# Ten input products of the mixing stage take raw weights and the normalised residual, in whole F32

## The chip, the cores and the metric

The kernel runs on one core of one Trainium2 chip, as one program. The metric is the device time of one execution in microseconds (us), and of several executions the median. The engines are named as the profile names them: PE multiplies matrices, PEld is PE's loading of the stationary operand, DVE, ACT and POOL work element by element, SP issues most of the DMA transfers.

## The reference, cut to what matters

One inference step of a decoder trunk with two layers, on 256 prompt tokens and 8 x 4 sample tokens; the kernel treats these 288 tokens as one set (NT = 288). A layer is

```python
x  = LN(alpha*x + 0.5*SwiGLU_1(x))            # ffn1, width 2816
z  = x @ W_in                                 # 1024 x 3584, the mixing stage's input product
z_rw, z_hg, z_cm = split(z, [1024, 1024 + 2048])
o  = concat[rwkv7(z_rw), hgrn2(z_hg), chunk_gmlp(z_cm)] @ W_out
x  = LN(alpha*x + o)
x  = LN(alpha*x + 0.5*SwiGLU_2(x))            # ffn2
...
q, fz, i, og = split(z_hg, 4)                 # HGRN2: 4 heads of 128 features
f = lb + (1 - lb)*sigmoid(fz);  log_f = log(max(f, 1e-30));  k = 1 - f
o = linear recurrence of silu(q), k, i, log_f;  o = rms(o)*norm_g*silu(og)
u, v = split(z_cm, 2)                         # gMLP: gelu(u), layer norm of gelu(v), causal mix
```

All of it is in float32. HGRN2's recurrence decays by products of f over tokens, so its inputs are wanted precisely.

## The kernel before

Activations lie feature-major: eight chunks of 128 features, each [128, 288]. A dense product yields 256 output features at a time, two PSUM accumulators `d` of [128, 288] (or 290 columns). Its weights come in blocks of 512 x 256 (`raw`, 512 KB, one DMA by SP at L347). W_in is fourteen such products of two blocks in each layer: four for RWKV (`rw_z`, called z here), and ten "background products" for HGRN2 and the gMLP: f, q, v, o with two each and cu, cv.

**Split products.** PE multiplies in F32R, a reduced form of float32. To keep precision, `prep` (L338) splits each block: ACT copies `raw` to `wh` in F32R, and DVE (for some blocks POOL) subtracts to get the low part `wl`. The moving side is split likewise into x-high and x-low (`newx`). `block` (L374) then issues three matmuls for each 128 x 128 piece (chunk k, column half c): wl by x-high, wh by x-high, wh by x-low. One product of 256 columns has 16 pieces, so 48 matmuls. `weights` keeps two blocks prepared ahead.

**The norm is applied after the product.** The product's operand x is (u - m) g, not yet divided by the deviation. `zfix` (L449) applies the norm to each result: it copies two extra columns (`cc<-d`), multiplies by the tokens' 1/deviation (`y<-d,rho`), and adds the shift (`y<-nu,cc,y`), all on DVE; sigmoid, gelu or copy on ACT and the gate on DVE follow, with cc as bias. The norm's output itself (`ax`, times ALPHA, for the residual sum after mixing) is made by `residual_g` (L696): per chunk `ax<-ax,rho` and `ax<-ax,nu` on DVE and `ax<-ax,ga` on ACT.

**Order.** The tile framework places each engine's instructions in one in-order stream by priority: trace order less the credit that `prio` gives (`PR`, L1782). In `mix` (L1689) the four z products come first. Then `go` runs the chains of `CHAINS` (L1778) in rounds: `pre` and `prompt` (RWKV for the prompt: decay, keys, a blocked inverse with doubling sizes), `sample`, `scan` (HGRN2's decay products with the matrices hA), `hmix`, `hsam`, `cm`, and others. After each step of a chain, `fill` takes a step (two pieces) of the background products, in the order `ORDER = ('f1', 'q0', 'f0', 'q1', 'cu', 'v1', 'cv', 'v0', 'o1', 'o0')`. `residual_g` is a chain of its own, `res`, last in the rounds. After the chains comes the output product (`mix_w_out`), split as the others, whose operand chunks 2 to 5 need HGRN2's results `hgO`.

**Who splits.** `PLO = {'z': (), 'f': (0,), 'q': (0,), 'v': (1,), 'c': (0,), 'o': (0,)}` names the blocks whose low part POOL makes: one of the two blocks of every background product, so ten a layer. Buffers: three each of `raw`, `wh`, `wl`, four PSUM banks `d`.

Names met below: `shp` transposes the token shift of RWKV, `pb` sums the squares of keys (from `rn`), `pD`, `pE`, `pR` belong to the prompt's inverse, `pns`, `poS` to the samples, `hot` turns HGRN2's outputs to feature-major, `cO` is the gMLP's mix (from `cM`), `hs` loads HGRN2's carried sample states (SP, L1523), `plg` is a small plain F32 product of the gate's lora.

Of the kernel before, what the change touches and what calls it, by code (L numbers as in the profile page):

```python
# [38 lines left out]
class Trunk:  # L39
# [80 lines left out]
    def consts(self):  # L120
# [34 lines left out]
        # causal masks over [s, t]: t > s and t >= s  # L155
# [5 lines left out]
        # block-merge masks: ml[b][t, s] and mt[b][s, t]  # L161
# [13 lines left out]
        # the same for blocks of 64 tokens, in rows of (block parity, token)  # L175
# [19 lines left out]
        # sample block masks over [(h,s), (h,t)], blocks of four tokens  # L195
# [9 lines left out]
        # the same with the rows of head h at the place of head (h + 2) % 4  # L205
# [3 lines left out]
        # row -> batch within a 32-token group, and row -> parity of its head  # L209
# [10 lines left out]
        # sums over a head's 64 rows into 32 equal rows, and their spreading back  # L220
# [11 lines left out]
        # a token's row in each group of 32; minus one at odd rows  # L232
# [3 lines left out]
        # two heads' inclusive sample blocks in either half of the rows  # L236
# [17 lines left out]
        # a token's row in each group of 32, for either pair of heads  # L254
# [3 lines left out]
        # the first four rows repeated for each batch  # L258
# [3 lines left out]
        # token -> batch, and a token's row in each group of 32  # L262
# [4 lines left out]
        # reset points of the running sums: token 0 of each chunk  # L267
# [70 lines left out]
    def prep(self, spec):  # L338
        """A block of weights, loaded and split into high and low parts."""
# [15 lines left out]
    @staticmethod  # L355
    def blocks(w, n0, nk, pool=()):
        return [(*w, tuple(range(k, min(k + 4, nk))), n0, i in pool) for i, k in enumerate(range(0, nk, 4))]
# [16 lines left out]
    def block(self, spec, x, res, first, last):  # L374
        """A block's share of a product."""
# [13 lines left out]

    def dense_g(self, w, n0, x, nk, pool, res):  # L390
# [11 lines left out]
    def dense_by(self, w, n0s, x, groups):  # L402
        """Several products, each group of chunks through all of them before the next."""
# [7 lines left out]
    def fill(self, n=1):  # L411
        """Goes on with the products in the background by n steps."""
# [18 lines left out]
    def hilo(self, r, name, n=NT):  # L431
        """Rows of high and low parts in turn, of equal rows."""
# [5 lines left out]
    def newx(self, nt):  # L438
        """Operand tiles of a product's moving side: eight 128-row chunks, high and low parts."""
# [9 lines left out]
    def zfix(self, ps, st, nm):  # L449
        """A product's two column blocks, and their biases, with the norm's scale (and shift) applied."""  # L450
# [148 lines left out]
    def final(self, po, m6, coef, g, square, i):  # L599
        """The last norm, in rows of tokens, and the outputs; the last rows are the prompt's end and the samples."""  # L600
# [6 lines left out]
        def rows(j, c):  # L607
            """A chunk, times the norm's gain, in rows of tokens."""
# [40 lines left out]
        # the mean's rest as rows of high, low and high parts  # L649
# [34 lines left out]
    def final_load(self, l):  # L684
        """The last norm's shift in each row, and its gain in (negated) rows of high, high and low parts."""
# [10 lines left out]
    def residual_g(self, pend):  # L696
        """The norm's output itself, times ALPHA for the next residual sum."""
# [9 lines left out]
    def residual_x(self):  # L707
        """The same, and operand tiles of it."""
        x = self.newx(NT)
        for c, _ in enumerate(self.residual_g(self.ln_pend)):  # L710
            self.act(x[0][c], self.ax[:, c])
            self.sub(x[1][c], self.ax[:, c], x[0][c].bitcast(F32), self.eng("xl"))
        return x

# [5 lines left out]
    def load_x(self, specs):  # L720
        """The operand tiles of the inputs; both loads in halves of the features, and the first weights between."""
# [24 lines left out]
    def rw_z(self, l, q, x, st):  # L746
# [41 lines left out]
    def rw_pre(self, l, q, zs):  # L788
# [3 lines left out]
        # lora products  # L792
# [3 lines left out]
        else:  # L796
            # tanh(x) = 2 sigmoid(2 x) - 1
# [19 lines left out]
        # running sums of the log decay (in units of -exp(-0.5)), centred in each chunk  # L817
# [17 lines left out]
        # keys  # L835
# [459 lines left out]
    def unit(self, l, n0, x, st, nm, fin):  # L1295
# [4 lines left out]
        for c in range(2):  # L1300
            fin(c, y[c], cb[c])
# [531 lines left out]
```

## Time and profile before

| what | value |
|---|---|
| median of 3 runs (lowest, highest) | 1374.07 us (1373.8, 1381.42) |
| span of the profiled execution | 1379.8 us |
| mean granted clock of PE | 0.969 |
| busy: PE, PEld, DVE, ACT, POOL | 1308.3, 1255.1, 1009.8, 663.8, 274.1 us |
| mixing stage of layer 0, from the first z product to the output product's end | 234 to 486 us |
| the same of layer 1 | 911 to 1155 us |

The span runs from the first to the last instruction of the profiled execution; the page gives no further time of its own for it, and it lies between the lowest and the highest of the three runs. An engine is busy while one of its arithmetic instructions runs. The granted clock is the share of PE's full clock that the throttle let it have (1.00 is 2.4 GHz, 0.50 is 1.2 GHz).

### The profile page before, as it was taken

What the parts mean: (1) busy time and instruction counts of PE and PEld (TensorE: products, weight loads), DVE (VectorE), ACT (ScalarE), POOL (GpSimd) and SP (SyncE); (2) the same over time, 40 slices, a digit from 0 to 9 for tenths busy, and PEclk for the clock granted to TensorE, in tenths of its full rate; (3) what the DMA queues carried; (4) which work ended last, traced back from release to release, by engine and by line L of the source; (5) the groups of instructions that cost most, each with busy time, mean ns of one, the idle gap of its engine ahead of it and who ended that gap; (6) DMA issues with size and microseconds to landing.
All of it is one profiled execution on the core that took longest, in us unless ns stands there. A gap on an engine that the chain in (4) does not pass through costs nothing.

```text
span 1379.8 us, 27635 instructions
## 1 busy us (share of the span) xinstructions
PE 1308.3 (95%) x11161; PEld 1255.1 (91%) x11162; DVE 1009.8 (73%) x1844; ACT 663.8 (48%) x1052; POOL 274.1 (20%) x381
## 2 busy tenths in 40 slices
PE   7999999898987999999999999998889889999998
PEld 6999999877876999999999999997778789999997
DVE  3555448977877998774698775599986889977643
ACT  4454435762345554443465443368333645544433
POOL 9200001435554100000100000033464421000002
PEclk9999999987997999999999999999999889999999
DMA  5655554531123655554455555554212544555551
GB/s 175 187 168 168 162 165 150 154 106 34 48 86 113 187 156 158 165 168 153 155 168 167 167 156 161 167 160 131 78 31 71 149 124 145 168 161 161 175 168 58
DMA packets 208158, 194.12 MB, mean 141 GB/s; under 512 B 15911, under 2 KB 206363, under 8 KB 208030
## 3 DMA queue, kind: packets, MB, share of 16 engines
q1 hardware_dynamic: 207326, 190.91, 44.9%
q0 software_dynamic: 608, 1.31, 0.4%
q8 instruction: 88, 1.44, 0.4%
q14 instruction: 40, 0.33, 0.1%
q10 hardware_dynamic: 96, 0.13, 0.1%
HBM read 185.10 MB, written 7.22 MB: 139 GB/s over the span
## 4 chain that ended last, share of the span: by engine, by line
PE 79%; DVE 14%; issue 3%; ACT 2%; POOL 1%; DMA 0%; POOLq 0%; SPq 0%; DVEq 0%; ACTq 0%
PE d L97 71%; DVE wl L65 2%; DVE hgO L77 1%; ACT wh L62 1%; DVE yrw L77 1%; DVE hgQ L77 1%; PE pA L97 1%; DVE hR L65 1%; DVE hAT L94 1%; PE hO L97 0%; PE hA L97 0%; DVE ax L65 0%; PE pD L97 0%; POOL hgP L65 0%; DVE hL L65 0%
## 5 line engine op out<-in xcount | busy, mean ns | idle before, releaser
L97 PE MATMUL d<-x,wh 128*128 128x290 f32 (+1 forms) x3968 | 824.0, 301 | 2.5 <-DVE x L77 2.5
L97 PEld LDWEIGHTS d<-x,wh 128*128 128x128 f32 x3968 | 653.3, 192 | 9.8 <-DVE x L77 4.3
L97 PE MATMUL d<-x,wl 128*128 128x290 f32 (+1 forms) x1984 | 602.5, 304 | 16.2 <-ACT x L62 12.4
L62 ACT ACTIVATE wh<-raw 128x1024 fp32r<-128x1024 f32 x344 | 357.2, 1039 | 456.1 <-PE d L97 312.1
L65 DVE TENSOR_TENSOR wl<-raw,wh 128x1024 fp32r<-128x1024 f32 x324 | 395.1, 1220 | 239.4 <-ACT wh L62 238.1
L97 PEld LDWEIGHTS d<-x,wl 128*128 128x128 f32 x1984 | 380.5, 192 | 21.5 <-ACT x L62 15.5
L97 PE MATMUL d<-h,wh 128*128 128x288 f32 x1408 | 282.0, 296 | 0.0
L97 PEld LDWEIGHTS d<-h,wh 128*128 128x128 f32 x1408 | 226.2, 188 | 0.2
L97 PE MATMUL d<-h,wl 128*128 128x288 f32 x704 | 207.8, 295 | 0.0
L65 POOL TENSOR_TENSOR lnv<-lnq,lnq 128x288 f32<-128x288 f32 x6 | 8.2, 1375 | 848.7 <-ACT lnq L62 848.7
L97 PEld LDWEIGHTS d<-h,wl 128*128 128x128 f32 x704 | 132.5, 188 | 0.2
L65 POOL TENSOR_TENSOR wl<-raw,wh 128x1024 fp32r<-128x1024 f32 x20 | 50.0, 2502 | 66.3 <-ACT wh L62 66.3
L62 ACT ACTIVATE h<-sg 128x288 fp32r<-128x288 f32 x88 | 38.1, 435 | 24.5 <-DVE sg L65 20.9
L62 ACT ACTIVATE sg<-yg,ccg 128x288 f32<-128x288 f32 x66 | 34.3, 528 | 29.9 <-DVE yg L77 29.9
L62 ACT ACT_TABLE_LOAD x37 | 47.5, 1283 | 1.4 <-PEq L1821 0.8
L65 DVE TENSOR_TENSOR h<-sg,h 128x288 fp32r<-128x288 f32 x88 | 39.6, 452 | 5.6 <-ACT h L62 5.6
L77 DVE SCALAR_TENSOR_TENSOR ax<-d,ax 128x288 f32<-128x288 f32 x48 | 21.4, 452 | 29.4 <-PE d L97 29.4
L77 DVE SCALAR_TENSOR_TENSOR yu<-nu,ccu,yu 128x288 f32<-128x288 f32 x66 | 33.9, 514 | 0.8
L77 DVE SCALAR_TENSOR_TENSOR yg<-nu,ccg,yg 128x288 f32<-128x288 f32 x66 | 33.8, 515 | 0.8
L62 ACT ACTIVATE lnq<-ax 128x288 f32<-128x288 f32 x48 | 20.9, 435 | 26.2 <-DVE ax L77 26.0
L77 DVE SCALAR_TENSOR_TENSOR sg<-yu,ccu,sg 128x288 f32<-128x288 f32 x66 | 33.3, 509 | 0.0
L65 DVE TENSOR_TENSOR yu<-d,rho 128x288 f32<-128x288 f32 x66 | 29.5, 448 | 0.0
(499 smaller groups left out, 1355.2 us busy)
## 6 DMA issues: line engine op xcount, KB each, us to landing
raw<-in_ffn_w_in SPq DMA_DIRECT2D x176, 512.0 KB
raw<-in_ffn_w_out SPq DMA_DIRECT2D x80, 512.0 KB
raw<-in_mix_w_in SPq DMA_DIRECT2D x56, 512.0 KB
raw<-in_mix_w_out SPq DMA_DIRECT2D x12, 512.0 KB
raw<-in_ffn_w_out SPq DMA_DIRECT2D x16, 256.0 KB
hs<-in_state_hgrn SPq DMA_DIRECT2D x8, 512.0 KB
out_hgrn_state_sample<-hs SPq DMA_DIRECT2D x8, 512.0 KB
raw<-in_mix_w_out SPq DMA_DIRECT2D x8, 256.0 KB
```

The lines of the kernel that those rows point to most:

```text
L62: self.nc.scalar.activation(out, in_, func, **kw)
L65: (eng or self.nc.vector).tensor_tensor(out, a, b, op=op)
L77: self.nc.vector.scalar_tensor_tensor(out, a, s, b, op0=op0, op1=op1)
L94: self.nc.vector.copy_predicated(out, mask.bitcast(I16), data)
L97: self.nc.tensor.matmul(out, lhsT, rhs, start=start, stop=stop)
```

## The change

`prep` returns the raw block when asked for "raw": no `wh`, no `wl`. A new generator `whole` multiplies it by `ax` in plain F32, one matmul instruction for each piece in place of three, over 288 columns. All ten background products of each layer use it. Since `ax` is the norm's output times ALPHA, `zfix` falls away for them: ACT and DVE read the PSUM accumulator itself, with the scale 1/ALPHA and no bias. `ax` must now be complete before the background starts: `residual_g` moves from its chain `res` into `rw_z`, two chunks after each z product. The table `PLO`, the chain `res` and a switch `RES` that was off are gone. The four z products, both FFNs and the output product stay split.

```diff
@@ prep
         for a, b in zip(runs, runs[1:]):
             src = self.I[name][l][ks[a] * 128:(ks[b - 1] + 1) * 128, n0:n0 + 256]
             nc.sync.dma_start(raw[:, a:b], src.rearrange("(c p) n -> p c n", p=128))
+        if pool == "raw":
+            return raw
         hi = self.wp.tile([128, 4, 256], F32R, tag="wh", name=f"wh{nc.next_id()}", bufs=B["wh"])
...
+    def whole(self, w, n0, x, nk, res):
+
+        res += [self.dps() for _ in range(2)]
+        for spec in self.blocks(w, n0, nk, "raw"):
+            raw = self.weights(spec)
+            for c in range(2):
+                for k, kk in enumerate(spec[2]):
+                    self.mm(res[c][:, :NT], raw[:, k, c * 128:(c + 1) * 128], x[:, kk], kk == 0, kk == nk - 1)
+                    if k % 2:
+                        yield
...
+        res = self.residual_g(self.ln_pend)
         for u in range(4):
             y, cb = self.zfix(self.dense(("mix_w_in", l), u * 256, x, KC, PLO["z"]), st, f"rw{l}{u}")
+            next(res), next(res)
...
-        yield from self.dense_g(("mix_w_in", l), n0, x, KC, PLO[nm[0]], res)
-        y, cb = self.zfix(res, st, f"{nm}{l}")
-        for c in range(2):
-            fin(c, y[c], cb[c])
...
+        yield from self.whole(("mix_w_in", l), n0, self.ax, KC, res)
+        for c in range(2):
+            fin(c, res[c][:, :NT])
...
-                a, op = (sc, ALU.mult) if cb is None else (cb, ALU.add)
-                self.hput(lambda o, s: self.stt(o, y[:, s], a, sg[:, s], op, ALU.mult), tile_(dst), 2 * u + c)
+                self.hput(lambda o, s: self.stt(o, y[:, s], sc, sg[:, s], ALU.mult, ALU.mult), tile_(dst), 2 * u + c)
...
-            "res": (lambda: self.residual_g(self.ln_pend),),
...
-PLO = {'z': (), 'f': (0,), 'q': (0,), 'v': (1,), 'c': (0,), 'o': (0,)}
+PLO = {'z': ()}
```

The scheduler then sets the instructions in another order at many places; three of them follow. `x` and `d` with their numbers are operand chunks and accumulators, `raw` the unsplit block.

PE at the start of the background in layer 0, before, from the end of the first product's block to the shift's transpose `shp`, the next transposes and the second block (eight pieces of three matmuls stand ahead of `shp`):

```order
L97 MATMUL d_3436<-x_2116,wl_3443 128x290
L97 MATMUL d_3436<-x_2116,wh_3441 128x290
L97 MATMUL d_3436<-x_2120,wh_3441 128x290
L101 MATMUL shp_3370<-ident,sh_2968 72x128
L101 MATMUL cwp_3384<-ident,cws_3381 128x128 x4
L97 MATMUL d_3434<-x_2118,wl_3452 128x290
```

The same place now, from the last z product's last matmul:

```order
L97 MATMUL d_3292<-x_2122,wh_3330 128x290
L97 MATMUL d_3458<-ax,raw_3462 128x288 x4
L97 MATMUL d_3460<-ax,raw_3462 128x288 x4
L101 MATMUL shp_3394<-ident,sh_2968 72x128
L101 MATMUL cwp_3408<-ident,cws_3405 128x128 x4
L97 MATMUL d_3458<-ax,raw_3465 128x288 x4
```

The 24 split matmuls ahead of `shp` have become eight whole ones, the same eight pieces.

PE in layer 0 where the prompt's inverse (pD, pE, pR), HGRN2's scan (hA, hAs) and the samples (pns, poS) alternate, before:

```order
L97 MATMUL hA_4306<-hR_4281,ones 128x512
L97 MATMUL hAs_4310<-hR_4281,ones 128x64
L97 MATMUL d_4493<-x_2120,wh_4362 128x290
L97 MATMUL d_4493<-x_2116,wl_4364 128x290
L97 MATMUL d_4493<-x_2116,wh_4362 128x290
L97 MATMUL pD_4322<-X_3741,DE_3740 64x64 x16
L97 MATMUL pE_4339<-DE_3740,X_3741 64x64 x16
L97 MATMUL pns_4373<-ub_4131,ex_3914 128x512
L97 MATMUL poS_4383<-idc,exq_4264 128x32
L97 MATMUL hA_4410<-hR_4281,hL_4280 64x64 x16
```

And now:

```order
L97 MATMUL hA_4070<-hR_4045,ones 128x512
L97 MATMUL hAs_4074<-hR_4045,ones 128x64
L97 MATMUL d_4005<-ax,raw_3894 128x288 x2
L97 MATMUL d_4007<-ax,raw_3894 128x288 x4
L97 MATMUL pD_4082<-X_3614,DE_3613 64x64 x16
L97 MATMUL pE_4099<-DE_3613,X_3614 64x64 x16
L97 MATMUL d_4005<-ax,raw_4009 128x288 x2
L97 MATMUL pns_4123<-ub_3930,ex_3758 128x512
L97 MATMUL poS_4129<-idc,exq_4032 128x32
L97 MATMUL hA_4152<-hR_4045,hL_4044 64x64 x16
```

Three split matmuls (one piece) stood between these links of the chains; now eight whole ones (eight pieces) do, and the background lies further back in the program: from `pb` to the last product of the prompt's chain PE has 58 pieces before and 79 now.

SP's issues at the end of the background in layer 0, with the semaphores that each waits for, before (`hs` are the carried states, `raw` from `in_mix_w_out` the output product's weights):

```order
L347 DMA raw_5771<-in_mix_w_out 128x4x256 [waits DMAHW3_49,DMAHW2_49,DVE_49]
L1523 DMA hs_5327<-in_state_hgrn 128x8x128 [waits PE_49]
L1127 DMA out_rwkv_state_prompt<-rwSo_5268 64x4x64 [waits DVE_49]
L1523 DMA hs_5329<-in_state_hgrn 128x8x128 [waits PE_49]
L1523 DMA hs_5331<-in_state_hgrn 128x8x128 [waits DMAHW4_49]
L1523 DMA hs_5333<-in_state_hgrn 128x8x128 [waits DMAHW5_49,DMASW6_49]
```

And now:

```order
L347 DMA raw_5208<-in_mix_w_out 128x4x256 [waits DMAHW4_49,DMAHW3_49,DVE_49]
L1135 DMA out_rwkv_state_prompt<-rwSo_4816 64x4x64 [waits DVE_49]
L347 DMA raw_5241<-in_mix_w_out 128x4x256 [waits DMAHW2_49,DMAHW1_49,PE_49]
L1529 DMA hs_4857<-in_state_hgrn 128x8x128
L1529 DMA hs_4859<-in_state_hgrn 128x8x128
L1529 DMA hs_4861<-in_state_hgrn 128x8x128
L1529 DMA hs_4863<-in_state_hgrn 128x8x128 [waits DMAHW5_49]
```

The four state loads now all stand behind a weight load that waits for PE, since a raw block is free only when PE has multiplied by it, no longer when ACT and DVE have split it.

## Rows read from the trace of the kernel before

**Rows 1.** The page, part 1 (busy time, share, instructions) and part 4 (ending chain by engine).

```profile
PE 1308.3 (95%) x11161; PEld 1255.1 (91%) x11162; DVE 1009.8 (73%) x1844; ACT 663.8 (48%) x1052; POOL 274.1 (20%) x381
...
PE 79%; DVE 14%; issue 3%; ACT 2%; POOL 1%; DMA 0%; POOLq 0%; SPq 0%; DVEq 0%; ACTq 0%
```

**Rows 2.** Layer 0 mixing by windows: us, busy PE/PEld/DVE/ACT/POOL (x), PEclk, DMA share, GB/s.

```profile
301.00:326.00 25.00, 24.89 (x196) 19.40 (x197) 13.09 (x40) 4.97 (x12) 7.23 (x9) 0.53 0.21 64
...
345.00:399.00 54.00, 51.74 (x915) 45.91 (x910) 38.67 (x74) 20.27 (x34) 26.33 (x23) 1.00 0.21 59
399.00:441.00 42.00, 29.22 (x238) 25.84 (x238) 35.96 (x53) 21.94 (x39) 24.73 (x22) 0.83 0.44 127
...
sum 252.00, PE 223.90 PEld 199.78 DVE 203.44 ACT 127.53 POOL 105.97; mean PE 31.98 PEld 28.54 DVE 29.06 ACT 18.22 POOL 15.14
```

**Rows 3.** The same of layer 1's mixing stage, 911 to 1155 us.

```profile
977.00:991.00 14.00, 13.10 (x190) 10.37 (x191) 12.61 (x43) 4.79 (x12) 3.37 (x7) 1.00 0.14 41
...
sum 244.00, PE 213.11 PEld 191.67 DVE 209.82 ACT 126.91 POOL 103.34; mean PE 30.44 PEld 27.38 DVE 29.97 ACT 18.13 POOL 14.76
```

**Rows 4.** A window of split FFN products.

```profile
540.00:560.00 20.00, 20.00 (x151) 20.00 (x150) 15.54 (x31) 8.80 (x12) 0.00 (x0) 1.00 0.54 164
```

**Rows 5.** A plain F32 product, `plg`: PE's timeline, then the tile (min/median/max ns).

```profile
272.33 0.65 PE L97 MATMUL plg<-sgx,wg 128*128 128x288 f32 x2
...
L97 PE MATMUL plg<-sgx,wg x8: 406/406/510, 272.0 to 949.6; 128*128 128x288 f32 x8
```

**Rows 6.** PE's waits, layer 0, 234 to 441 us: total us, times, longest.

```profile
PE d L97 <- ACT x L62: 6.2, 1, 6.2
PE cO L97 <- DVE cM L65: 5.7, 1, 5.7
PE shp L101 <- POOL sh L773: 4.6, 1, 4.6
PE pb L97 <- DVE rn L77: 2.6, 1, 2.6
```

**Rows 7.** The same, layer 1, 911 to 1110 us; its other three read as above.

```profile
PE cO L97 <- DVE cM L65: 4.3, 1, 4.3
```

**Rows 8.** Stretches of half clock, as windows (the sum is of all eight).

```profile
263.00:270.00 7.00, 4.97 (x22) 4.66 (x23) 5.03 (x16) 6.12 (x9) 1.37 (x7) 0.52 0.40 128
300.50:324.00 23.50, 22.89 (x182) 17.57 (x183) 13.59 (x41) 4.11 (x9) 7.23 (x9) 0.50 0.22 68
413.00:423.00 10.00, 7.82 (x38) 6.67 (x39) 5.10 (x11) 4.85 (x10) 3.31 (x5) 0.50 0.57 172
...
sum 80.50, PE 65.60 PEld 56.59 DVE 52.05 ACT 31.60 POOL 34.16; mean PE 8.20 PEld 7.07 DVE 6.51 ACT 3.95 POOL 4.27
```

**Rows 9.** Tiles `wl` and `yq`: ns min/median/max, first and last start us.

```profile
L65 DVE TENSOR_TENSOR wl<-raw,wh x324: 691/1224/2852, 9.3 to 1355.6; 128x1024 fp32r<-128x1024 f32 x162
L65 POOL TENSOR_TENSOR wl<-raw,wh x20: 2352/2445/2965, 251.9 to 1072.2; 128x1024 fp32r<-128x1024 f32 x20
...
L65 DVE TENSOR_TENSOR yq<-d,rho x8: 439/441/450, 280.7 to 1000.3; 128x288 f32<-128x288 f32 x8
L77 DVE SCALAR_TENSOR_TENSOR yq<-nu,ccq,yq x8: 505/519/2609, 281.2 to 1001.2; 128x288 f32<-128x288 f32 x8
```

**Rows 10.** Timeline of POOL, then of DVE, 252.4 to 252.6 us.

```profile
251.94 2.69 POOL L65 TENSOR_TENSOR wl<-raw,wh 128x1024 fp32r<-128x1024 f32 x1 [1.06 <-ACT wh L62]
...
252.30 2.65 DVE L77 SCALAR_TENSOR_TENSOR yrw<-nu,ccrw,yrw 128x288 f32<-128x288 f32 x1
```

**Rows 11.** Timeline of SP's queue, 395 to 425 us.

```profile
419.85 2.35 SPq L1523 DMA_DIRECT2D hs<-in_state_hgrn  x3
```

More of the change, by code (lines that the diff above doesn't have):

```diff
@@ L356, in blocks @@
     def blocks(w, n0, nk, pool=()):
-        return [(*w, tuple(range(k, min(k + 4, nk))), n0, i in pool) for i, k in enumerate(range(0, nk, 4))]
+        return [(*w, tuple(range(k, min(k + 4, nk))), n0, pool if pool == "raw" else i in pool)
+                for i, k in enumerate(range(0, nk, 4))]
     def weights(self, spec):
@@ L705, in residual_g @@
             yield
[L707 to L713, printed above, removed]
     def residual(self):
@@ L1293, in hput, with unit, hg_units @@
         f(self.hsm(out)[:, h], slice(T, NT))
-    def unit(self, l, n0, x, st, nm, fin):
+    def unit(self, l, n0, nm, fin):
         res = []
-        yield from self.dense_g(("mix_w_in", l), n0, x, KC, PLO[nm[0]], res)
-        y, cb = self.zfix(res, st, f"{nm}{l}")
+        yield from self.whole(("mix_w_in", l), n0, self.ax, KC, res)
         for c in range(2):
-            fin(c, y[c], cb[c])
-    def hg_units(self, l, q, x, st, sc):
-        hg = {}
+            fin(c, res[c][:, :NT])
+    def hg_units(self, l, q):
+        hg, sc = {}, 1.0 / ALPHA
         def tile_(n):
@@ L1313, in f_, with fin @@
         def f_(u):
-            def fin(c, y, cb):
+            def fin(c, y):
                 h = 2 * u + c
                 if q["lb"] is None:
-                    self.hput(lambda o, s: self.act(o, y[:, s], AF.Sigmoid, cb, sc), tile_("P"), h)
+                    self.hput(lambda o, s: self.act(o, y[:, s], AF.Sigmoid, scale=sc), tile_("P"), h)
                 else:
                     sg = self.e(f"fs{l}{h}")
-                    self.act(sg, y, AF.Sigmoid, cb, sc)
+                    self.act(sg, y, AF.Sigmoid, scale=sc)
                     self.hput(lambda o, s: self.ts(o, sg[:, s], q["olb"][:, h:h + 1], q["lb"][:, h:h + 1],
@@ L1325, in silu, with fin @@
         def silu(dst, u):
-            def fin(c, y, cb):
+            def fin(c, y):
                 sg = self.e(f"qs{self.nc.next_id()}")
-                self.act(sg, y, AF.Sigmoid, cb, sc)
+                self.act(sg, y, AF.Sigmoid, scale=sc)
                 if dst == "O":
@@ L1331, in fin @@
                     self.act(sg, sg, scale=q["hg_norm_g"][:, h:h + 1])
-                a, op = (sc, ALU.mult) if cb is None else (cb, ALU.add)
-                self.hput(lambda o, s: self.stt(o, y[:, s], a, sg[:, s], op, ALU.mult), tile_(dst), 2 * u + c)
+                self.hput(lambda o, s: self.stt(o, y[:, s], sc, sg[:, s], ALU.mult, ALU.mult), tile_(dst), 2 * u + c)
             return fin
         def v_(u):
-            def fin(c, y, cb):
-                self.hput(lambda o, s: self.act(o, y[:, s], AF.Identity, cb, sc), tile_("V"), 2 * u + c)
+            def fin(c, y):
+                self.hput(lambda o, s: self.act(o, y[:, s], scale=sc), tile_("V"), 2 * u + c)
             return fin
@@ L1353, in hg_units @@
         for n, o in (("cv", 13), ("cu", 12)):
-            r[n] = (o, lambda c, y, cb, n=n: self.act(tile2(n)[:, c], y, AF.Gelu, cb, sc))
+            r[n] = (o, lambda c, y, n=n: self.act(tile2(n)[:, c], y, AF.Gelu, scale=sc))
         for n in ORDER:
             o, f = r[n]
-            self.wq += self.blocks(("mix_w_in", l), o * 256, KC, PLO[n[0]])
-            self.bg.append((f"{n}{l}", self.unit(l, o * 256, x, st, n, f)))
+            self.wq += self.blocks(("mix_w_in", l), o * 256, KC, "raw")
+            self.bg.append((f"{n}{l}", self.unit(l, o * 256, n, f)))
     def hg_scan(self, l):
@@ L1694, in mix @@
         self.rw_shift_out(l, sh)
-        if RES:
-            with self.prio("res0"):
-                x, st = self.residual_x(), None
-        sc = 1.0 / ALPHA if RES else 1.0
         self.loras(l, q)
         cw = self.cm_prep(l)
-        self.hg_units(l, q, x, st, sc)
+        self.hg_units(l, q)
         def go(*gens):
@@ L1765, in mix @@
             "houts": (lambda: self.hg_out(l, mt(1), 2), "hsam", "o0", "o1"),
-            "res": (lambda: self.residual_g(self.ln_pend),),
         }
-        go(*[(chain(n, *ch[n]), f, n) for n, f in CHAINS if not (RES and n == "res") and n not in LATE])
+        go(*[(chain(n, *ch[n]), f, n) for n, f in CHAINS if n not in LATE])
         m = m[0]
@@ L1778 @@
 CHAINS = [('prompt', 1), ('pre', 3), ('rst', 1), ('hsam', 1), ('posts', 1), ('hst', 1), ('hmix', 1), ('sample', 1),
-          ('cm', 1), ('post', 1), ('houts', 1), ('hout', 1), ('hou0', 3), ('scan', 1), ('res', 0)]
+          ('cm', 1), ('post', 1), ('houts', 1), ('hout', 1), ('hou0', 3), ('scan', 1)]
 LATE = ()
-PR = {'prep': 250, 'posts': 450, 'hou0': -50, 'scan': 400, 'hsam': -150, 'post': -400, 'res': 50, 'scan.4': 20,
+PR = {'prep': 250, 'posts': 450, 'hou0': -50, 'scan': 400, 'hsam': -150, 'post': -400, 'scan.4': 20,
       'cm.1': 200, 'q1.0': -7, 'hmix': 20, 'hst.6': 100, 'sample.0': -20, 'hmix.7': -20, 'posts@1': -400,
@@ L1793 @@
 B = {'m4': 19, 'e': 5, 'a2': 11, 'raw': 3, 'wh': 3, 'wl': 3, 'y': 6, 'Z': 2, 'cc': 6, 'Ab': 1, 'd': 4, 'ds': 0}
-RES = False
-PLO = {'z': (), 'f': (0,), 'q': (0,), 'v': (1,), 'c': (0,), 'o': (0,)}
+PLO = {'z': ()}
 ORDER = ('f1', 'q0', 'f0', 'q1', 'cu', 'v1', 'cv', 'v0', 'o1', 'o0')
```

## The prediction, made before the changed kernel ran

> **What bounds the kernel now.** I read the page's first and fourth parts, then the windows of the two mixing stages (the only places that the change touches), then PE's waits inside them, and last the stretches in which PE's clock is at half. The page says PE: busy for 95% of the span, 79% of the chain that ended last [rows 1]. The windows say the same of the stage, with less certainty: in layer 0, PE is busy 223.9 of 252 us, in layer 1, 213.1 of 244 [rows 2, 3]. So PE is idle for 28 and 31 us, the only pool from which waits can be won back. DVE, at 203 and 210 us of the same stages, is not far behind it: a stage that both engines nearly fill, in which now one and now the other ends the wait. The parts differ. In the prompt's inverse (345 to 399 us) PE is busy 51.7 of 54 us; what is added there is paid in full. In the stage's end (399 to 441 us) it is busy only 29.2 of 42 [rows 2].
>
> PE's waits of layer 0, longest first: 6.2 us for the last operand of the output product (`x` from ACT, behind HGRN2's outputs), 5.7 for the gMLP's operand `cM` from DVE, 4.6 for the token shift `sh` from POOL, 2.6 for `rn` from DVE [rows 6]; layer 1 has the same four, with 4.3 for `cM` [rows 7]. And in eight stretches of the two stages, 80.5 us together, PE was granted half its clock, 1.2 GHz [rows 8]; each of them began in or soon after a wait of PE. The largest, 23.5 us from 300.5 us on, came after the wait for `rn`. Layer 1 shows its price: the same work from `pb` on (some 190 matmul records) took 25 us in layer 0 at 0.53 of the clock and 14 us in layer 1 at 1.00 [rows 2, 3], though layer 1 also waited 2.6 us before it.
>
> **The change, term by term.** Durations are of the profiled execution, 1379.8 us long, which is 5.7 us above the median of the three runs, 1374.07; differences are taken from it and set against the median.
>
> *PE's own work.* A split product piece is three F32R matmuls. In a window that they fill without a gap, 151 took 20.00 us [rows 4], so one is 0.1325 us and a piece 0.397. The plain F32 form stands in the trace only as `plg`: each product leaves two records, and two records back to back span 0.65 us with one lasting 0.406 [rows 5]; the second record added 0.65 - 0.41 = 0.24 us, so a product is 2 x 0.24 = 0.485 us. The piece grows by 0.0875 us. Ten products of 16 pieces in two layers are 320 pieces: **+28 us**, 14 in each layer. That is exact only if a run of whole products keeps this pitch; the trace has no longer run of that width with a new weight for each product. The bounds: a piece at the whole duration of two records one after the other, 0.81 us, would be absurdly dear (+132 us), and is excluded since PE overlaps them in the row itself; I take 0.45 to 0.53, which is +17 to +43.
>
> The Trainium skill speaks against this count: "Perfetto Trace Analysis", section Engine Utilization, gives the array's rate in FP32_LOW_HIGH as half of the usual one. By it a piece would be 0.24 us, and PE would save some 50 us instead of paying 28; but the trace has two records of 0.24 us for one `plg` product [rows 5], and the measurement decides.
>
> *Splitting.* Twenty blocks a layer are no longer split: 20 copies on ACT, ten subtractions on DVE at 1.22 us (12 us) and ten on POOL at 2.45 us (24.5 us) [rows 9]. *The norm after the product:* DVE drops a multiplication of 0.44 and an addition of 0.52 us for each of 20 column halves [rows 9], and a small copy: some 20 us by medians, and more where additions met POOL. So DVE loses some 32 us a layer or more of about 205. None of this is PE's time; it is worth only the PE waits that DVE or POOL ended last. Which of them go:
> - `shp` waits for POOL's `sh` (4.6 us). POOL's weight splits no longer stand ahead of it, and the eight pieces ahead of it on PE now last 3.9 us as against 3.2. I leave 0.5 us: -4.1 in each layer.
> - `cO` waits for DVE's `cM` (5.7 and 4.3 us). DVE has no splits and no corrections of `yo` there, and PE reaches `cO` later by its longer background: all of it goes, -5.7 and -4.3.
> - `pb` waits for `rn`, in a chain that DVE, ACT and PE pass between them. DVE is lighter; I leave 1 us: -1.6 each.
> - The smaller waits of a microsecond or two each (for hR, uv and the like): half, -2 and -3.8.
> - The wait for the output product's operand (6.2 us each) stays. The carried states that feed it are loaded at the end, three of them in one batch at 419.85 us [rows 11], and SP's order now sets all four behind a weight load that waits for PE; the relief of DVE and the later start cancel as far as the trace tells.
>
> Sum of waits: -13.4 in layer 0 and -13.8 in layer 1, **-27 us**. Bounds: nothing gained (DVE's place is taken by the next link of the same chain, most of which passes through PE itself), or all 59 us of idle time but the 12.4 for the operand, -47.
>
> *Clock.* Where a wait goes, the slow stretch behind it should go too. In half-clock stretches PE did 65.6 us of work [rows 8], which at full clock would be some 33 less if all of it ran at PE's rate, and by the lengths of the stretches up to 40: that is the limit. I count the stretches after `shp` (7 us at 0.52 in layer 0, so 3.4 lost, and half of that in layer 1, where it is half as long), after `cO` (4 each of the 5 lost in ten us at half clock from 413 us on) [rows 8], and after `pb` in layer 0 the 11 us by which it differs from layer 1, at 0.6 since layer 1 shows that the same wait can pass without it: 6.6. **-20 us**, between 0 and -40.
>
> *The moved residual.* Eight chunks, each with two DVE operations of the size of yq's multiplication (0.44 us [rows 9]) and one of ACT, are pulled ahead of the background. PE computes four z products meanwhile, 192 matmuls x 0.1325 = 25 us; before, ten of the 16 DVE operations already ran there. The six others, some 2.7 us, take the place of DVE work that POOL's collisions cost there: an addition on DVE took 2.65 us beside a POOL split of 2.69 us [rows 10], against a median of 0.52 [rows 9]. I cost it at nothing; without that cover the first background product starts up to 3 us later in each layer.
>
> The Trainium skill has that collision as a rule: "SBUF — State Buffer", section on the two separate sides, says that a DVE instruction with two SBUF inputs and a POOL instruction that reads SBUF shut each other out for their whole length. The rows agree: the addition from SBUF reaches 2.61 us, while the multiplication that reads PSUM never passes 0.45 [rows 9]. By the rule the gates of Q and O, which now read PSUM, escape POOL too, some 4 us a layer on DVE, which the sum leaves out.
>
> *DMA.* The same bytes move. A raw block is now held from its load until PE has used it, with three buffers as before, and two blocks last 32 x 0.485 = 15.5 us of PE's time at the least: I see no starving there, since the background is spread over 150 us.
>
> **Sum:** +28 - 27 - 20 = -19. From the median: 1374 - 19 = **1355 us** (the profiled execution: 1361).
>
> **The rivals.**
> *A, the waits go and the clock isn't regained.* PE's clock may fall at other waits as well as at these. Then +28 - 27 = +1: **1375**. For it: layer 1 had the same 2.6 us wait before `pb` and kept its clock, so wait and clock aren't tied one to one. Against: two thirds of the half-clock time follows a wait that the change should shorten.
> *C, PE runs through.* The chain-passing waits all go, since between two links there are now eight pieces (3.9 us) where there was one (0.4), and with them two thirds of the clock's 40: 28 - 47 - 27 = -46, **1328**. For it: DVE sheds a sixth of its work in a stage where it is nearly as full as PE. Against: the inverse had next to no idle time to give, 2.3 of 54 us [rows 2].
> *B, slower: the background's end is late.* The background is pushed back, 79 pieces instead of 58 between `pb` and the prompt chain's end: 38 us instead of 23, in the stretch where PE has no idle time. O's gates end later, the state loads stand behind a weight load that waits for PE, and the wait for the operand grows from 6.2 to 12 us in each layer, with a half-clock stretch behind it as before. The waits then give 10 us in all and the clock 10: 28 + 12 - 10 - 10 = +20, **1394**. It decides when the states land later than some 17 us after the last background product, or when `cM` and `sh` simply arrive as late behind other work. For it: SP's order, and the exact count on PE. Against: before, the loads were already issued late, at 419.85 us [rows 11].
> *D, whole products are twice as fast as I count*: if the second record of `plg` were no part of one product but a product itself, a piece would be 0.24 us, PE would shed (0.397 - 0.24) x 320 = 50 us, and of the waits and the clock at most 30 would come on top, as PE would then wait for the others: 1374 - 50 - 30 = **1294**. Against it: the program has four such products, and the trace eight records [rows 5]. It is the page's rule above that speaks for it.
>
> **How the numbers follow.** Chances: forecast 0.40, A 0.22, C 0.19, B 0.17, D 0.02. The forecast's own spread is some 12 us either way. One per cent, 13.7 us, is about what a measurement of this kernel can tell from no change: faster is below 1360.3, slower above 1387.8. Three quarters of the forecast's spread lie below 1360.3; with C and D, 0.30 + 0.19 + 0.02 = 0.51. Within: a quarter of the forecast and A, 0.32. Slower: B, 0.17. The range from 1318 to 1392 takes in A, nearly all of C and the nearer half of B, and leaves out D and the farther half of B, with the lower end of C and of the pitch's bound some 0.17.
>
> **What would show it.** In the profile after: whole products `d<-ax,raw` back to back at 0.485 us a piece (0.45 or 0.53 moves the sum by 11 to 15); PE's busy time up by 28 us less what the clock gives; the waits at `shp` and `cO` gone, the wait of `d` for `x` still near 6 us; the windows from `pb` on near 14 us in both layers at a clock of 1.00; DVE down by 60 to 70 us over both layers. The prediction fails if PE's idle time in the stages stays near 59 us (then A or B), if the granted clock stays at 0.97 or falls, or if raw blocks come late, which would show as waits of `d<-ax,raw` for DMA.

## The result, and the profile after

| | before | after |
|---|---|---|
| median (lowest, highest), us | 1374.26 (1373.8, 1381.42), 4 runs | 1355.35 (1353.02, 1356.73), 4 runs |
| ratio, 95% interval | | 0.9843 [0.9809, 0.9877] |
| span of the profiled execution, us | 1379.8 | 1355.0 |
| mean granted clock of PE | 0.969 | 0.986 |

The change makes the kernel 18.9 us faster by the medians, 1.4%, and 1.6% by the ratio, which is worked out from all runs; the forecast was 1355, 19 us faster. Of 44 later executions of the kernel before, 12 took 1378.8 to 1383.2 us, at a granted clock of 0.966 to 0.971, and the others 1370.8 to 1376.6. The page of the kernel after, its parts 1 and 4, against [rows 1]:

```profile
PE 1310.4 (97%) x10842; PEld 1222.9 (90%) x10842; DVE 908.0 (67%) x1704; ACT 622.6 (46%) x1014; POOL 226.3 (17%) x361
...
PE 85%; DVE 7%; DMA 3%; issue 3%; ACT 1%; SPq 1%; POOL 1%; POOLq 0%; ACTq 0%; DVEq 0%
```

PE is busy for as long as before in a span 25 us shorter, DVE for 102 us less; in the chain DVE's share has halved. A new link stands there, DMA with 3%.

In the later runs a time lies some 1.7 us above its span, so the profiled execution of before was that of 1381.42 us, 7 us above the median and not 5.7, as its span had seemed to say. The kernel before was therefore profiled once more (1374.22 us, span 1372.5). Windows of that execution, each layer's mixing stage in two parts, cut at the end of the gMLP's product `cO` (columns: window, length, busy time of each engine, PEclk, DMA share, GB/s). The second part, like the ends 486 and 1155 in the table of before, reaches to the end of the norm that follows the output product, some 9 us after that product's last matmul:

```profile
234.50:409.10 174.60, 153.80 (x1932) 136.97 (x1931) 146.02 (x282) 89.14 (x153) 88.24 (x95) 0.96 0.31 90
409.10:478.80 69.70, 61.19 (x435) 56.49 (x436) 58.47 (x103) 38.05 (x79) 20.61 (x17) 0.87 0.49 150
904.90:1079.00 174.10, 152.97 (x1932) 136.01 (x1931) 151.12 (x290) 88.56 (x149) 86.33 (x91) 0.96 0.29 87
1079.00:1148.40 69.40, 60.42 (x437) 55.85 (x436) 58.46 (x103) 37.52 (x78) 18.55 (x12) 0.88 0.51 149
```

The same four stretches of the kernel after:

```profile
233.70:398.60 164.90, 162.03 (x1795) 127.52 (x1795) 97.30 (x218) 68.60 (x135) 58.59 (x81) 1.00 0.31 92
398.60:469.00 70.40, 57.26 (x412) 52.14 (x411) 56.80 (x98) 37.71 (x78) 24.32 (x21) 0.88 0.54 156
895.20:1058.60 163.40, 161.51 (x1795) 127.31 (x1795) 99.76 (x226) 68.35 (x130) 57.29 (x77) 1.00 0.30 89
1058.60:1129.40 70.80, 56.70 (x413) 51.50 (x412) 56.74 (x98) 37.88 (x78) 23.64 (x16) 0.90 0.53 153
```

All of the gain lies ahead of `cO`: 9.7 us in layer 0 and 10.7 in layer 1. What follows has become 0.7 and 1.4 us longer, although it has less to do: before, some twelve pieces of the background stood behind `cO` in each layer, and now four, so about 4 us of PE's work has moved ahead of the cut. Ahead of `cO` PE is now idle for 2.9 and 1.9 us, where it was idle for 20.8 and 21.1, and its clock is whole. Behind `cO` its idle time has grown, from 8.5 and 9.0 us to 13.1 and 14.1.

PE's waits of the whole kernel after (us in total, times, longest), against [rows 6, 7]:

```profile
PE hp L97 <- DMA hs<-in_state_hgrn: 6.8, 3, 4.7
PE hot L101 <- DVE hon L65: 5.0, 2, 3.1
PE hp L97 <- POOL hqm L65: 4.7, 1, 4.7
PE d L97 <- ACT x L62: 4.2, 2, 2.1
...
PE pb L97 <- DVE rn L77: 1.9, 2, 0.9
...
PE shp L101 <- POOL Z L771: 0.4, 1, 0.4
PE shp L101 <- POOL sh L781: 0.4, 1, 0.4
```

`shp` went from 4.6 us a layer to 0.4, `pb` from 2.6 to 0.9, `cO` is no longer in the list. Instead PE waits for `hp`, the product of the samples with the carried states. In layer 1 the list puts these waits, 6.0 us, to the loads of the states; in layer 0 it puts the first, 4.7 us, to `hqm`, the other operand, which POOL makes, and only the last 0.7 to the loads. That the loads came last there too, the chain shows (layer 0, from the last background product to `hp`: start, us, what):

```profile
401.18 0.99 PE d L97 x4
402.16 0.02 issue
402.18 0.37 SPq L347
402.55 0.05 issue
402.60 0.51 SPq L1529
...
405.84 8.34 DMA hs<-in_state_hgrn
414.18 0.14 issue
414.31 1.69 PE hp L97 x53
```

The last background product ends, that frees a raw block, SP issues the weight load that waited for it, and only then the four state loads behind it in the queue; the last lands 12 us after that product. With an earlier `hqm` PE would only have come sooner to the wait for that load. Before, the batch went out late too, at 419.85 us [rows 11], but PE, which had waited for `cO`, came to `hp` only at 426.1 us, and no wait for `hp` stands in its list. The wait of `d` for `x`, which the prediction had left at 6.2 us a layer, is 2.1.

### The profile page after: what moved, and what is told of

Its sections match the earlier page's. It is cut to its first block, busy times and chain, and to the rows that moved or that the text cites. A ratio compares the mean times of both kernels' runs of the same rounds, so it can differ in the third digit from the quotient of the medians.

```text
span 1355.0 us, 26724 instructions
## 1 busy us (share of the span) xinstructions
PE 1310.4 (97%) x10842; PEld 1222.9 (90%) x10842; DVE 908.0 (67%) x1704; ACT 622.6 (46%) x1014; POOL 226.3 (17%) x361
## 4 chain that ended last, share of the span: by engine, by line
PE 85%; DVE 7%; DMA 3%; issue 3%; ACT 1%; SPq 1%; POOL 1%; POOLq 0%; ACTq 0%; DVEq 0%
PE d L97 74%; DMA hs<-in_state_hgrn 1%; PE hA L97 1%; DVE wl L65 1%; PE pX L97 1%; DMA raw<-in_mix_w_out 1%; DVE x L65 1%; ACT wh L62 1%; PE pE L97 1%; PE pD L97 1%; DVE ax L65 1%; DMA raw<-in_ffn_w_in 1%; DVE zs L77 0%; SPq L1529 0%; DVE OT L65 0%
## 5 line engine op out<-in xcount | busy, mean ns | idle before, releaser
L97 PE MATMUL d<-x,wh 128*128 128x290 f32 (+1 forms) x3328 | 680.3, 299 | 3.9 <-DVE x L65 2.1
L97 PEld LDWEIGHTS d<-x,wh 128*128 128x128 f32 x3328 | 542.2, 190 | 8.1 <-DVE x L77 3.6
L65 DVE TENSOR_TENSOR wl<-raw,wh 128x1024 fp32r<-128x1024 f32 (+1 forms) x304 | 366.2, 1204 | 255.0 <-ACT wh L62 254.0
L62 ACT ACTIVATE wh<-raw 128x1024 fp32r<-128x1024 f32 (+1 forms) x304 | 315.1, 1036 | 422.9 <-PE d L97 268.9
L97 PE MATMUL d<-x,wl 128*128 128x290 f32 (+1 forms) x1664 | 497.6, 299 | 6.9 <-ACT x L62 4.2
L97 PEld LDWEIGHTS d<-x,wl 128*128 128x128 f32 x1664 | 316.3, 190 | 8.8 <-ACT x L62 7.2
L97 PE MATMUL d<-ax,raw 128*128 128x288 f32 x640 | 174.3, 415 | 0.0
L97 PEld LDWEIGHTS d<-ax,raw 128*128 128x128 f32 x640 | 115.3, 190 | 30.4 <-issue 2.3
```

What stands on the lines that cost most here:

```text
L62: self.nc.scalar.activation(out, in_, func, **kw)
L65: (eng or self.nc.vector).tensor_tensor(out, a, b, op=op)
L97: self.nc.tensor.matmul(out, lhsT, rhs, start=start, stop=stop)
```

## The experiments

Ratios are to runs of the kernel before that were taken together with the experiment's; differences from the changed kernel are between medians. In any stretch, length is PE's work at the whole clock, plus its idle time, plus what half clock costs. The work is taken as PE's busy time less half of the part that fell into half clock, and that half is the cost of the clock.

**The kernel before once more** (`before_again`), unchanged.

> The kernel before, unchanged, profiled once more. Theory 1 (the account: time = PE's work + PE's idle time + what half clock costs) takes the 23.5 us of half clock behind `pb` in layer 0 for an accident of the one profiled execution, which was 5.7 us above the median: a usual execution spans 1370 to 1374 us and has 50 to 70 us of half clock in the two mixing stages in place of 81. Rival: the half clock belongs to that wait in layer 0 and stands there again, 23 us long, with a span of 1378 or more.

It took 1374.22 us, its span 1372.5, with 61 us of half clock in the two stages, as theory 1 had it. The stretch behind `pb` of layer 0, that [rows 8] have at half clock for 23.5 us, in this execution:

```profile
301.20:324.70 23.50, 21.62 (x376) 17.13 (x376) 21.70 (x47) 7.65 (x19) 12.31 (x12) 1.00 0.25 71
```

PE did twice the instructions in the same time, at the whole clock. So the half clock there belongs to some executions, not to the kernel; the 6.6 us that the prediction took for its end were not to be had from the median.

**PE's work taken back** (`f32r3`).

```diff
-                    self.mm(res[c][:, :NT], raw[:, k, c * 128:(c + 1) * 128], x[:, kk], kk == 0, kk == nk - 1)
+                    wr, xr = raw[:, k, c * 128:(c + 1) * 128], x[kk // 4][:, kk % 4]
+                    for j in range(3):
+                        self.mm(res[c][:, :NT], wr, xr, kk == 0 and j == 0, kk == nk - 1 and j == 2)
```

(`raw` and `x` are here the F32R copies by ACT, and the scale behind the product is 1/(3 ALPHA).)

> The changed kernel, but each whole F32 product is three F32R matmuls on the same two high parts (ACT still copies each weight block and each residual chunk to F32R; the low parts are left out of the result). PE's work is as before the change, DVE's and POOL's relief stays. Theory 1: PE paces the stage, so its 24 to 28 us of added work come off, less 5 to 10 us of waits that return: 1335 us (1325 to 1345). Rival (DVE, POOL and the chains set the end, PE's added work was hidden): 1350 to 1358.

1324.66 us, ratio 0.9633 [0.9593, 0.9673]: 30.7 us less than the changed kernel, just below the range of theory 1. The windows of layer 0, up to `cO` and behind it:

```profile
233.80:386.50 152.70, 147.29 (x1927) 131.36 (x1927) 98.99 (x218) 83.89 (x157) 59.44 (x81) 1.00 0.34 99
386.50:452.80 66.30, 59.58 (x441) 54.53 (x440) 56.57 (x98) 38.12 (x80) 23.43 (x21) 0.92 0.57 166
```

Over both stages PE's work is 22 us less, half clock costs 2 us less, and idle time is 8 us less. So the added work was paid in full, and it is 22 of the 30.7 us. The idle time is two things. Ahead of `cO` 6.5 us came back (4.8 to 11.3 over both layers), as theory 1 had it. Behind `cO` 14 us went (27.2 to 13.1): there the state loads go out earlier than in the changed kernel, from 386 us on, and some eight pieces more of each layer's background stand there to fill the time.

**PE's work raised** (`wide`). In the last chunk the operand starts 52 columns early, so its share of the sum stands in wrong columns.

```diff
-                    self.mm(res[c][:, :NT], raw[:, k, c * 128:(c + 1) * 128], x[:, kk], kk == 0, kk == nk - 1)
+                    o, xf = (52, x.rearrange("p c n -> p (c n)"))
+                    a0 = kk * NT - (o if kk == KC - 1 else 0)
+                    self.mm(res[c][:, :NT + o], raw[:, k, c * 128:(c + 1) * 128], xf[:, a0:a0 + NT + o], kk == 0,
+                            kk == nk - 1)
```

> The changed kernel with each whole product 52 columns wider (340 in place of 288, the surplus unused): 52 x 4 columns at 2.4 GHz are 87 ns a piece, the very surplus that the prediction put on a whole piece over a split one. Theory 1: nothing hides it while PE paces: +22 to +28 us, 1380 (1375 to 1385). Rival (PE's added work is hidden beside the chains): 1356 to 1365.

1379.39 us, ratio 1.0028 [1.0008, 1.0049]: +24.0 of the 27.5 us added. Up to `cO`, at the whole clock in both kernels, the stages are 12.3 and 14.1 us longer, 26.4 together. The longest run of whole products in PE's timeline, of the kernel after:

```profile
383.11 13.85 PE L97 MATMUL d<-ax,raw 128*128 128x288 f32 x56
```

and of this one:

```profile
392.70 16.27 PE L97 MATMUL d<-ax,raw 128*128 128x340 f32 x56
```

56 records are 28 products: 0.495 us each at 288 columns, 0.581 at 340, so 86 ns for 52 columns.

**The splits put back** (`ghost_split`): `prep` makes `wh` and `wl` as before, returns `raw`.

```diff
-        if pool == "raw":
-            return raw
         hi = self.wp.tile([128, 4, 256], F32R, tag="wh", name=f"wh{nc.next_id()}", bufs=B["wh"])
...
+        if pool in ("raw", "rawp"):
+            return raw
...
-PLO = {'z': ()}
+PLO = {'z': (), 'f': (0,), 'q': (0,), 'v': (1,), 'c': (0,), 'o': (0,)}
```

> The changed kernel with the twenty splits of a layer put back (ACT copies, ten subtractions on DVE, ten on POOL as before), though nothing reads them. Theory 1: a part of PE's waits returns with the load on POOL and DVE, shp's 4.6 us in each layer and some of cO's, with the clock behind them: 1370 us (1363 to 1380). Rival (with PE as full as it is now the splits hide beside it, the gain came from the norm no longer applied after the product): 1353 to 1359.

1376.32 us, ratio 1.0003 [0.9978, 1.0028]: +21.0, as much as the whole gain. It lies ahead of `cO`, 11.3 and 10.2 us: PE's idle time there rises from 4.8 to 21.1 us over both layers, and 10 us of half clock return. That is less than half of the way back to the 41.9 us of before. Two of PE's waits in it:

```profile
PE shp L101 <- POOL Z L772: 3.5, 1, 3.5
PE shp L101 <- POOL sh L782: 3.4, 1, 3.4
```

**The same, POOL free** (`ghost_dve`): all entries of `PLO` empty, so the twenty subtractions of a layer are DVE's.

> As the run with the splits put back (1376.3 us, 21 above the changed kernel), but all twenty subtractions of a layer on DVE and none on POOL. It tells whose load brought the waits back. Theory 1 (POOL's late results, as sh before shp, and its collisions with DVE): without POOL's subtractions at least half of the 21 us goes, 1364 us (1358 to 1368), though DVE carries 12 us a layer more. Rival (DVE's load is what counts): 1374 or more.

1361.56 us, ratio 0.9898 [0.9863, 0.9932]: 14.8 of the 21 us are gone, with 12 us more on DVE. The two waits:

```profile
PE shp L101 <- POOL Z L772: 0.5, 1, 0.5
...
PE shp L101 <- POOL sh L782: 0.4, 1, 0.4
```

So `shp` waited because POOL's weight splits stood ahead of the small copies that make `sh`, as the prediction had it.

**Only ACT's copies put back** (`ghost_act`): as above, without `lo` and its subtraction.

> The changed kernel with only ACT's twenty copies of a layer put back, and no subtraction at all; nothing reads the copies. ACT is busy about half of the stage. Theory 1: hidden, 1357 us (1354 to 1360). Rival (ACT's copies stand ahead of what the chains wait for, since ACT runs in order): 1363 to 1372.

1348.46 us, ratio 0.9803 [0.9766, 0.9841]: 6.9 us faster than the changed kernel, with more work in it. Neither theory had that. SP's queue in layer 0 of this kernel (start, us, what):

```profile
390.13 7.16 SPq L347 DMA_DIRECT2D raw<-in_mix_w_out  x5
397.33 0.51 SPq L1531 DMA_DIRECT2D hs<-in_state_hgrn  x1
399.58 0.60 SPq L1137 DMA_DIRECT2D out_rwkv_state_prompt<-rwSo  x1
400.23 2.57 SPq L1531 DMA_DIRECT2D hs<-in_state_hgrn  x3
```

With the copies the scheduler set another order at the stage's end, and the state loads went out 3 to 5 us earlier, ahead of the weight load. PE's idle time behind `cO` is 10.3 and 9.9 us, where it was 13.1 and 14.1. The other two runs with the splits have the same order there. Read against this kernel, the subtractions cost 13 us on DVE alone and 28 with half of them on POOL.

**The norm put back** (`ghost_norm`).

```diff
-        for c in range(2):
-            fin(c, res[c][:, :NT])
+        for c in range(2):
+            y = self.ep.tile([128, NT], F32, tag="y", name=f"y{nm}{l}{c}", bufs=B["y"])
+            self.nc.vector.tensor_copy(cc[:, c], res[c][:, NT - 2:NT])
+            self.mul(y, res[c][:, :NT], rho)
+            if nu is not None:
+                self.stt(y, nu, cc[:, c, 1:2], y, ALU.mult, ALU.add)
...
```

> The changed kernel with the norm's multiplication and addition after each background product put back on DVE (some 20 us a layer; the result is normalised twice, so it is not the reference's). Theory 1: in a stage where DVE is busy some 155 of 235 us this mostly hides; it costs where the gates end the chain at the stage's end: 1359 us (1355 to 1365). Rival (this was the relief that paid): 1366 to 1378.

1356.42 us, ratio 0.9861 [0.9821, 0.99]: +1.1 by the median. Its state loads too go out early, so the norm may cost up to 8 us, since `ghost_act` with that order is 7 us faster; from the first z product to `cO`'s end it is 166.3 us long in layer 0, against 164.9, and 166.1 in layer 1, against 163.4.

**The moved residual alone** (`moved_residual`), in the kernel before.

```diff
+        res = self.residual_g(self.ln_pend)
...
+            next(res), next(res)
...
-            "res": (lambda: self.residual_g(self.ln_pend),),
```

> The kernel before with one part of the change alone: the normalised residual is made beside the z products, two chunks after each, in place of the last chain. Products stay split. Theory 1 costs it at nothing: 1374 us (1370 to 1378). Rival (the six further DVE operations delay the corrections of z and with them the start of the background, 3 us a layer): 1380.

1372.26 us, ratio 0.9978 [0.9956, 0.9999]: nothing that counts.

**The norm's output as operand, still split** (`split_residual`), in the kernel before.

```diff
-RES = False
+RES = True
```

> The kernel before with its own switch set that makes the normalised residual, split into high and low parts, the operand of the background products: no norm after the product, but weights and operand still split, three F32R matmuls a piece. DVE sheds some 20 us a layer and gains up to 8 subtractions there or on POOL, and the background waits for them. Theory 1 (the splits on POOL and DVE are what the waits at shp and cO come from, and they stay): 1370 to 1380. Rival (applying the norm after the product was the costly part): 1355 to 1362.

1363.34 us, ratio 0.9907 [0.9877, 0.9937]: -10.5, between the two ranges and nearer to the rival. With the splits still there, the corrections by the norm are worth some 10 us, net of the splitting of the operand; without them, 1 to 8. So the reliefs don't simply add up.

**The state loads earlier** (`early_states`).

```diff
+    def hs_load(self, l):
+        self.hsS0 = []
+        for h in range(4):
+            s0 = self.m4([128, 8, 128], f"hs0{l}{h}")
+            self.hsS0.append(s0)
+            self.nc.sync.dma_start(s0, self.I["state_hgrn"][l, :, h].rearrange("b k v -> k b v"))
+        yield
...
+            "hsl": (lambda: self.hs_load(l), "scan", "prompt"),
```

> The changed kernel with the four loads of HGRN2's carried states issued as soon as the scan and the prompt's chain are done, ahead of the last background product's weights and of the output product's. In the changed kernel PE waits 5 to 7 us a layer for the sample product hp, whose states were loaded behind a weight block that waited for PE. Theory 1: this wait goes, and with it some of the half clock behind it: -8 to -14, 1345 us. Rival (what comes next at the same place, the operand chain on DVE, ends no earlier, or the last weight block now comes late): 1352 to 1360.

1363.45 us, ratio 0.9902 [0.9867, 0.9937]: 8 us slower than the changed kernel, above both ranges. SP's queue in layer 0:

```profile
387.11 3.21 SPq L1502 DMA_DIRECT2D hs<-in_state_hgrn  x3
390.37 3.69 SPq L1135 DMA_DIRECT2D out_rwkv_state_prompt<-rwSo  x1
394.10 0.61 SPq L1502 DMA_DIRECT2D hs<-in_state_hgrn  x1
394.82 1.50 SPq L347 DMA_DIRECT2D raw<-in_mix_w_in  x1
396.42 15.10 SPq L347 DMA_DIRECT2D raw<-in_mix_w_out  x8
```

and the waits of PE there, 384 to 445 us:

```profile
PE d L97 <- DVE x L65: 5.1, 2, 4.1
PE hot L101 <- ACT hos L62: 4.7, 1, 4.7
PE d L97 <- DMA raw<-in_mix_w_in: 2.3, 1, 2.3
```

The wait for `hp` went, and others came: a store that waits for DVE slipped between the state loads and held up the last weight block and, behind it, the output product's.

**The state loads earlier still** (`states_first`): the chain `hsl` needs only "v1".

> The changed kernel with the four loads of the carried states still earlier than in the run that had them ahead of the last weight block (1363.5 us; there a store that waits for DVE stood between them and held up that block): as soon as the second value product is done. Theory 1: PE's wait for hp goes and nothing stands behind the store, -5 to -10: 1348 us. Rival (the operand chain on DVE and ACT ends the stage, wherever the loads stand): 1353 to 1364.

1344.68 us, ratio 0.977 [0.973, 0.9811]: 10.7 us faster than the changed kernel, with the same arithmetic; the fastest version here that leaves nothing out. SP's queue in layer 0:

```profile
345.28 2.58 SPq L1286 DMA_DIRECT2D out_rwkv_state_sample<-no  x4
347.95 4.23 SPq L1502 DMA_DIRECT2D hs<-in_state_hgrn  x4
352.28 31.49 SPq L347 DMA_DIRECT2D raw<-in_mix_w_in  x5
```

PE's idle time behind `cO` falls by 5 us in layer 1; in layer 0 it stays at 13.5, since the wait for `hp` gives way to one of 7.8 us for DVE's `OM`. About as much comes from the clock: 17 us of half clock in the two stages, where the changed kernel has 31. How far the loads themselves brought that about isn't shown.

**One F32R matmul a piece** (`one_f32r`): `f32r3` without the loop over `j`.

> As the run with three F32R matmuls a piece (1324.7 us), but one, of the two high parts alone; the low parts are left out, so this is a product of less precision than either kernel's. PE sheds another 2 x 0.151 x 320 = 97 us in the stages. Theory 1: PE no longer paces, the chains on DVE and ACT and the stage's end do, and about half is got back: 1275 us (1260 to 1290). Rival (PE's account holds in full): 1230.

1319.34 us, ratio 0.9588 [0.9553, 0.9623]: 5.3 us less than with three, where half of 97 was expected; both theories expected far more. Its longest waits of PE:

```profile
PE cO L97 <- POOL cvn L65: 19.9, 2, 9.9
PE hot L101 <- DVE hon L65: 12.9, 4, 5.8
```

and its windows of layer 0, up to `cO` and behind it:

```profile
233.90:384.40 150.50, 118.04 (x1646) 100.75 (x1647) 100.13 (x222) 90.83 (x167) 59.35 (x84) 0.89 0.38 116
384.40:446.50 62.10, 54.92 (x400) 49.58 (x401) 49.10 (x94) 30.24 (x69) 22.89 (x19) 0.88 0.47 139
```

PE idles for 32 us ahead of `cO` and loses clock besides. The account by PE's work ends somewhere between `f32r3` and this run: from there on the chains set the time.

## Why the prediction was right

**The sum** held, -19 against -18.9, and so did its frame: PE paces the stage. Added work was paid (`wide`, 24 of 27.5 us) and removed work came back (`f32r3`). That the sum fits to a fraction of a microsecond is luck, as its terms show.

**PE's own work** was put at +28 us. The pitch of whole products in an unbroken run was right: 0.485 us, in the longest run 0.495 with its ends. Measured over both stages the work is +22: busy time less half of what fell into half clock is 203.0 and 201.5 us in the execution of before, 213.4 and 213.1 after (+10.4, +11.6). The term took both sides from unbroken runs. In the stage the pieces stand in short groups between other products, and by the starts in the traces (ahead of `cO`, at the whole clock) a split matmul took 0.150 us on average, not the 0.1325 of the unbroken window [rows 4], and a whole product 0.519. So three split matmuls came out 0.05 us dearer than forecast and a whole product 0.03, and the piece grew by 0.07 us, not by 0.0875.

The 28 whole products of the longest run take 13.85 us in 56 records, 0.247 us a record, and 52 more columns cost 86 ns a product. The Trainium skill's rate for FP32_LOW_HIGH ("Perfetto Trace Analysis", section Engine Utilization) is half of the usual one, by which 288 columns take an estimated 0.24 us. The runs agree with that for one record; a whole product has two, so rival D is ruled out. Another page of the Trainium skill, "FP8 and Floating Point Precision", section TensorE Precision Notes, has true FP32 take four passes. The runs agree: four times 52 columns at 2.4 GHz are 87 ns.

**The waits** were put at -27 us; PE's idle time in the stages fell by 27.4 (29.3 and 30.1 to 16.0 each). That agreement is made of two errors. Ahead of `cO` the idle time fell by 37: not only `shp`, `cO` and `pb` went, but nearly all the small waits of the chains too, some 15 us, which the prediction halved to 6. Behind `cO` it rose by 10: there the prediction left 6.2 us a layer unchanged ("the relief of DVE and the later start cancel"), and SP's order, which it had printed, made a new wait. That is rival B's mechanism, at 5 us a layer in place of 6 with the other waits kept. What took the 37 us away is known in part: put back one at a time, the splits return 16 of them (`ghost_split`), the norm 3 (`ghost_norm`), and PE's shorter work 6 (`f32r3`). The other 11 or so no run took apart: they may be reliefs that cover each other, or the new order of the instructions.

**Who ended the waits**: POOL more than DVE. `ghost_split` and `ghost_dve` show it for `shp` directly, and for 15 of the 21 us by time that the splits bring back.

DVE itself was relieved of more than was forecast: 103 us in the two stages, where 60 to 70 were expected. The gates of Q and O alone went from 27.5 us there to 9.6. Before, the 16 gates of Q took up to 2.34 us; with POOL's splits back in `ghost_split`, those that now read PSUM never took over 0.425, while the additions from SBUF that fell away had reached 2.61 [rows 9]. The Trainium skill's exclusive lock ("SBUF — State Buffer", section on the two separate sides) fits this. It doesn't explain one gate of Q in `ghost_dve`, which took 0.893 us beside a memset on POOL.

**The clock** was put at -20 us, and gave some 13 (half of PE's busy time in half clock: 23.8 us in the stages of before, 11.0 after). The 6.6 us behind `pb` belonged to the profiled execution. Of the 8 us counted behind `cO` some 5 came: the first stretch of half clock at or behind `cO` went from 10 us in each layer to 7 and 3, and the one that follows it, 10 us in each, stayed. The 5 us behind `shp` came. And two stretches that the sum had not counted went too, 3 us long in layer 0 and 7 in layer 1, ahead of `cO`. (By the lengths of the stretches, 61 us before and 31 after, the clock gave 15 us; by the busy time in them, 13.)

**The moved residual** at nothing was right (`moved_residual`), and raw blocks, held longer, didn't starve PE: no wait of `d<-ax,raw` for a DMA stands in the list. The prediction's margin for that was half of what it says: two blocks are 16 pieces, 7.8 us of PE's time, not 15.5.

So the three sizes were off by 6, 0 and 7 us, and the first and the last cancelled; within the waits two more errors did, of 10 us each. What the runs leave open is how much of the 13 us of clock follows from the waits. Ahead of `cO` the kernel after has 5 us of idle time over both layers and no half clock; `wide`, `ghost_norm`, `ghost_dve` and `f32r3`, with 3 to 11, have none either; `ghost_split`, with 21 and `shp`'s wait again, has 10 us of half clock there, and before, with 42, has 27.

## What to carry to other kernels

Where one engine is nearly full, count work and idle time of that engine separately: each microsecond of work added or removed was worth close to one here, as long as the chains had slack, and next to nothing once they had none (97 us removed gave 5). When a buffer's release moves from an early reader to a late one, as raw blocks here from ACT and DVE to PE, read what stands behind the next load in the DMA queue: moving four unrelated loads well ahead gave another 10.7 us, and moving them less far cost 8. Take the price of an instruction from the stage where it stands and not from an unbroken run. Take a clock term from more than one execution.

## What was not expected

A run with twenty more copies a layer on ACT was 6.9 us faster, and the one difference found is that the scheduler then put the state loads elsewhere. So a difference of a few microseconds between two versions of a scheduled program can be the order alone, and a probe that adds work has to be compared up to a common point ahead of it, not only by its time. And the same instructions behind `pb` ran at half clock for 23.5 us in one execution and at the whole clock in another, with the same wait before them.
